# Decoder layer on one core: x squared by contiguous adds two groups later, FFN2's first gate/up group in row form

## Chip, cores and metric

One core of a Trainium2 chip. The metric is device time in microseconds of one execution, lower is better.

## What is computed

One decoder layer on x of 256 tokens by 1024 features, float32. Each sub-layer is wrapped in RMSNorms:

```python
x = x + 0.5 * rmsnorm(swiglu(rmsnorm(x, g1), w_gate, w_up, w_down), g2)      # FFN1, 2816 wide
x = x + rmsnorm(concat(attention(h), pooling(h)) @ w_out, g)                 # mixer
x = x + rmsnorm(cross_attention(h, rmsnorm(mem, gm)) @ wo, g)                # 4 heads
x = x + 0.5 * rmsnorm(swiglu(rmsnorm(x, g3), w_gate, w_up, w_down), g4)      # FFN2, 2816 wide
# swiglu: (silu(h @ w_gate) * (h @ w_up)) @ w_down
```

The root of the norm ahead of a product is one factor for each token. The kernel multiplies the unnormalised x (times the gain) and applies the root to the result, so a group of products can start before the root is known.

## The kernel before, in words

**Split weights.** Every weight and every x is split in a high half (rounded to fp32r) and a low half (the rest), and a product is three matmuls: hi by hi, lo by hi, hi by lo. Weights arrive in the order of use, in units of eight 128x128 tiles (512 KB), loaded by SP, mostly two to a transfer, into one of four `wraw` buffers (L66). `_make` (L70) casts a unit on ScalarE (`whi`, L76) and subtracts on VectorE (`wlo`, L77). `get` (L120) hands the next tiles to TensorE and, at the start of unit u, makes all units up to u + 4 (`LEAD`), or as many as `pace` says. There are six `whi` and six `wlo` buffers.

**Two forms of product.** In column form a weight tile is stationary and x (256 tokens, or 512 columns of hi and lo side by side) streams: `group` (L219) computes two gate and two up chunks (f = 0 and 1) in two PSUM banks, k by k, twelve matmuls of 256 columns for each of eight k; `gate_up` (L564) computes a later f, one unit for the gate and one for the up half, each eight pairs of 256 and 512 columns (L574, L575). In row form a 128x128 piece of x is stationary and 512 columns of weights stream: `row_product` (L293), three matmuls at L298 to L300.

**Order.** TensorE runs in program order everywhere. Between `seam(True)` and `seam(False)` (L795) all engines do; elsewhere a planner arranges the other engines.

**Opening.** `start` (L469) loads x and the first four units in parts and splits them (L108, L111, L181, L184). Then it squares x in place on ScalarE (L497, two halves) and reduces over the chunks on VectorE, reading with a stride (L498), and computes four small factors (L500). FFN1's `group` follows, then f = 2, 3, ... `x_sums` (L514) reduces over the partitions by four matmuls against a column of ones (eight TensorE instructions) after the gate of f = 2, and takes the root. `opened` (L604), after the gate of f = 3, spreads the root over the partitions (L286, two matmuls, four instructions) and finishes the f so far: root, silu, product, split into `h`. Down steps begin after f = 5. `mem_rows` (L526) is a load of SP's queue, issued after f = 4, into the buffer that held x.

**Seam ahead of FFN2.** The cross-attention's output product ends with three units (`row_end`, L368; `row_sums`, L313): tile t = 0 (128 tokens) of both 512-wide halves, then t = 1. Each half's result is squared and summed on ScalarE (L324) and scaled into `y` on VectorE (L327). `row_root` (L336) takes the root, `row_add` (L345) adds y to x (`xt`), `x_turn` (L349) transposes 128x128 pieces of `xt` on TensorE (L353), and `x_hi` (L374, ScalarE) and `x_lo` (L378, VectorE) split them. With no filler work (`fillers` empty, this seam only) the transposes of t = 0 stand after the products, `middle` and `ahead` do the first chunks, and `before(j)` puts the transposes of t = 1 and the other splits between the k of FFN2's first `group`. There `rows_square` (L507) sums x squared for the root, `x_root` (L356) follows at f = 3 and `opened` at f = 4. One `wlo` is made on GpSimd.

Of the kernel before, what the change touches and what calls it, by code (L numbers as in the profile page):

```python
# [47 lines left out]
class Weights:  # L48
# [33 lines left out]
    def open_in_parts(self, n_units, load, split):  # L82
# [54 lines left out]
def build(nc, io, tiles_only=False):  # L137
# [230 lines left out]
    def row_end(parts, ks, weights, factor, nxt, pre, fillers):  # L368
# [12 lines left out]
        def products():  # L381
            st["w"].pace = [(LEAD, None)] * (LATE - 1) + [(LEAD - 1, None)]
# [9 lines left out]
            box["sums"] = row_sums(parts, ks, ws, 1, factor, box["later"])  # L392
            x_turn(0, range(4), small)
            x_turn(0, range(4, 8), small)

        def middle():
            r = box["r"] = row_root(box["sums"])
            if not fillers:
                x_hi(0, 0)
                row_add(1, slice(0, P), r)  # L400
                x_hi(0, 1)
                return
            for c in range(ND):
                x_hi(0, c)
            for i in range(2):
                row_add(1, quarter(i), r)
            box["later"][0]()
            for i in range(2, 4):
                row_add(1, quarter(i), r)
            for c in range(4):  # L410
                x_lo(0, c)
# [13 lines left out]
        def ahead():  # L425
            r = box["r"]
            x_turn(1, (0,), accum)
            row_add(1, slice(P, S), r)
            x_lo(0, 0)
            x_turn(1, (1,), accum)  # L430
            x_hi(1, 0)
            x_hi(1, 1)
            row_add(1, quarter(1), r)
            x_lo(1, 0)
            x_lo(0, 1)
            x_lo(1, 1)
            box["later"][0]()

        def before(j):
            if fillers and j == 1:  # L440
                k_flush()
            if j == 0 and not fillers:
                st["w"].pace = [(2, "dve"), (2, "pool"), (2, "dve"), (3, "dve"), (3, None), (3, None)]
            if j % 2 == 1 and j < 7 and not fillers:
                c = j + 1
                x_turn(1, (c, c + 1), accum)
                for k in (c, c + 1):
                    x_hi(0, k)
                    x_hi(1, k)
                if c < 6:  # L450
                    row_add(1, quarter(c // 2 + 1), box["r"])
                for k in (c, c + 1):
                    x_lo(0, k)
                    x_lo(1, k)
            if j in (2, 4, 6, 7):
                rows_square(st["xt"], st["xsum"], {2: 0, 4: 1, 6: 2, 7: 3}[j])

# [5 lines left out]
        if not fillers:  # L463
            pr.add(ahead)
        return before
# [3 lines left out]
    def start():  # L469
# [43 lines left out]

    def x_sums():  # L514

        ps = small("sums")
        for t in range(2):
            for i in range(2):
                nc.tensor.matmul(ps[:, t:t + 1], st["xsq"][:, i, t * P:(t + 1) * P], st["one"],
                                 start=i == 0, stop=i == 1)  # L520
# [40 lines left out]
    def ffn(n, X, before, aside, last):  # L561
# [40 lines left out]
        first = 2 if n == 1 else 3  # L602

        def opened():  # L604
            x_spread()
            for f, t in enumerate(early):
                finish(f, t)
# [6 lines left out]
        group([wg, wu] * 2, X, [0, 0, P, P], early.extend, before=before, hi_first=n == 1)  # L614
        seam(False)
        for f in range(2, NF):
            gate, up = gate_up(f, early.append if f < first + 1 else lambda t, f=f: finish(f, t))
            pr.add(*gate)
            if f == first:
                side(x_sums if n == 1 else x_root)  # L620
            if f == first + 1:
                side(opened)
            pr.add(*up)
# [504 lines left out]
```

## Time and profile before

| | us |
|---|---|
| three runs | 577.92, 578.73, 578.73 |
| median | 578.73 |
| the profiled execution | 580.79 |
| its span | 578.6 |
| TensorE busy (matmuls) | 565.5 (98%) |
| VectorE busy | 411.2 (71%) |
| ScalarE busy | 341.6 (59%) |
| DMA engines, mean share | 53% |

The durations come from the profiled execution. A matmul's duration contains its passage through the array, so the distance between the starts of two matmuls, not the duration, is what one of them costs. Lines are those of the kernel before.

### The profile page before, as it was taken

The page shows a single profiled execution, that of the slowest core. Times are in us where ns is not written, and L with a number is a line of the kernel's source. Part 1 is how long each engine was busy: PE and PEld are TensorE (multiplying, and loading weights), DVE is VectorE, ACT ScalarE, POOL GpSimd, SP SyncE. Part 2 cuts the span into 40 slices and gives each one's busy share as a digit, 9 for nine tenths or more (in the row PEclk, how much of TensorE's full clock was granted, in tenths as well). Part 3 has the DMA queues.
Part 4 walks back from the last instruction along what each step waited for, and adds up shares of the span by engine and source line. Part 5 has one row for each costly group of instructions (what it writes and reads, how often), then busy time and mean ns, then how long its engine had stood idle before and what let it go on. Part 6 is the DMA issues. An engine that isn't in the chain of part 4 may idle for free.

```text
span 578.6 us, 8485 instructions
## 1 busy us (share of the span) xinstructions
PE 565.5 (98%) x3304; PEld 496.7 (86%) x3304; DVE 411.2 (71%) x662; ACT 341.6 (59%) x613; POOL 20.0 (3%) x37
## 2 busy tenths in 40 slices
PE   8799999999999999999999999999999999999995
PEld 8788888888888899988899988879888888888884
DVE  5898666787776678984568676467796766766654
ACT  6588575555555656775359456358674555555543
POOL 0000000000000000450000000001000000000001
PEclk9899999999999999999999999999999999999998
DMA  8885686645646068264256624426655555545202
GB/s 298 310 344 182 254 281 227 217 159 206 204 163 216 18 237 287 79 218 147 72 187 246 219 113 146 146 72 222 253 195 184 202 180 185 200 164 218 74 1 73
DMA packets 29400, 107.04 MB, mean 185 GB/s; under 512 B 2096, under 2 KB 3248, under 8 KB 28976
## 3 DMA queue, kind: packets, MB, share of 16 engines
q1 hardware_dynamic: 28928, 106.14, 52.3%
q8 instruction: 26, 0.43, 0.3%
q10 hardware_dynamic: 432, 0.35, 0.2%
q14 instruction: 14, 0.11, 0.0%
HBM read 105.44 MB, written 1.05 MB: 184 GB/s over the span
## 4 chain that ended last, share of the span: by engine, by line
PE 92%; DVE 3%; DMA 2%; ACT 1%; issue 1%; DVEq 0%; SPq 0%
PE acc L575 13%; PE sm L575 13%; PE acc L298 10%; PE acc L300 9%; PE acc L299 9%; PE acc L574 7%; PE sm L574 7%; PE acc L173 3%; PE acc L174 3%; PE acc L175 3%; PE acc L234 2%; PE acc L232 2%; PE acc L260 2%; PE acc L262 2%; PE acc L261 2%; PE acc L227 2%
## 5 line engine op out<-in xcount | busy, mean ns | idle before, releaser
L77 DVE TENSOR_TENSOR wlo<-wraw,whi 128x1024 fp32r<-128x1024 f32 x183 | 223.7, 1231 | 76.9 <-ACT whi L76 76.4
L76 ACT CAST whi<-wraw 128x1024 fp32r<-128x1024 f32 x184 | 192.5, 1053 | 51.1 <-PE acc L300 41.5
L575 PE MATMUL acc<-xs,whi 128*128 128x512 f32 x320 | 115.9, 401 | 0.0
L575 PE MATMUL sm<-xs,whi 128*128 128x512 f32 x320 | 114.5, 398 | 0.0
L574 PE MATMUL acc<-xs,wlo 128*128 128x256 f32 x320 | 90.4, 282 | 3.1 <-DVE wlo L77 3.1
L574 PE MATMUL sm<-xs,wlo 128*128 128x256 f32 x320 | 90.1, 282 | 0.0
L575 PEld LDWEIGHTS acc<-xs,whi 128*128 128x128 f32 x320 | 60.7, 190 | 14.6
L575 PEld LDWEIGHTS sm<-xs,whi 128*128 128x128 f32 x320 | 60.1, 188 | 14.9
L298 PE MATMUL acc<-whi,h 128*128 128x512 f32 x176 | 69.0, 392 | 0.0
L300 PE MATMUL acc<-whi,h 128*128 128x512 f32 x176 | 68.7, 390 | 0.0
L299 PE MATMUL acc<-wlo,h 128*128 128x512 f32 x176 | 68.5, 389 | 0.0
L574 PEld LDWEIGHTS acc<-xs,wlo 128*128 128x128 f32 x320 | 60.8, 190 | 4.5 <-DVE wlo L77 3.3
L574 PEld LDWEIGHTS sm<-xs,wlo 128*128 128x128 f32 x320 | 60.5, 189 | 0.0
L579 ACT COPY cmb<-acc 128x256 f32<-128x256 f32 x40 | 14.9, 373 | 53.6 <-PE acc L575 53.4
L173 PE MATMUL acc<-xs,wlo 128*128 128x256 f32 x160 | 46.1, 288 | 0.0
L174 PE MATMUL acc<-xs,whi 128*128 128x256 f32 x160 | 45.2, 283 | 0.0
L175 PE MATMUL acc<-xs,whi 128*128 128x256 f32 x160 | 45.2, 283 | 0.0
L579 ACT COPY cmb<-sm 128x256 f32<-128x256 f32 x40 | 14.8, 371 | 50.6 <-PE sm L575 50.6
L300 PEld LDWEIGHTS acc<-whi,h 128*128 128x128 f32 x176 | 33.0, 188 | 7.3
L299 PEld LDWEIGHTS acc<-wlo,h 128*128 128x128 f32 x176 | 33.1, 188 | 7.1
L298 PEld LDWEIGHTS acc<-whi,h 128*128 128x128 f32 x176 | 33.0, 188 | 5.6
L232 PE MATMUL acc<-xs,whi 128*128 128x256 f32 x128 | 32.4, 285 | 0.8 <-ACT whi L108 0.8
(179 smaller groups left out, 896.5 us busy)
## 6 DMA issues: line engine op xcount, KB each, us to landing
wraw<-w SPq DMA_DIRECT2D x91, 1024.0 KB, 4.8
post<-post SPq DMA_DIRECT2D x4, 512.0 KB, 5.2
wraw<-w SPq DMA_DIRECT2D x7, 256.0 KB, 5.8
wraw<-w SPq DMA_DIRECT2D x2, 512.0 KB, 7.2
y<-memt SPq DMA_DIRECT2D x1, 1024.0 KB, 9.9
y<-mem SPq DMA_DIRECT2D x1, 1024.0 KB, 6.9
xt<-xt SPq DMA_DIRECT2D x1, 1024.0 KB, 6.8
out_dram<-y SPq DMA_DIRECT2D x4, 128.0 KB, 1.9
```

The lines of the kernel that those rows point to most:

```text
L76: self.nc.scalar.copy(hi, raw)
L77: eng.tensor_tensor(lo, raw, hi.bitcast(F32), op=ALU.subtract)
L173: nc.tensor.matmul(o, lo, X[:, :S], start=first, stop=False, skip_group_check=True)
L174: nc.tensor.matmul(o, hi, X[:, :S], start=False, stop=False, skip_group_check=True)
L175: nc.tensor.matmul(o, hi, X[:, S:], start=False, stop=last, skip_group_check=True)
L232: nc.tensor.matmul(o[i], hi, st[X][:, k, :S], start=first and i % 2 == 0, stop=False, skip_group_check=True)
L298: nc.tensor.matmul(o, a, hi, start=first, stop=False, skip_group_check=True)
L299: nc.tensor.matmul(o, a, lo, start=False, stop=False, skip_group_check=True)
L300: nc.tensor.matmul(o, b, hi, start=False, stop=last, skip_group_check=True)
L574: nc.tensor.matmul(ps[:, S:], lo, x[:, :S], start=k == 0, stop=False, skip_group_check=True)
L575: nc.tensor.matmul(ps, hi, x, start=False, stop=k == ND - 1, skip_group_check=True)
L579: nc.scalar.copy(c, ps[:, S:])
```

## The change

1. `start` no longer squares x. `x_squares` does so after the gate of f = 2 of FFN1: the same two squares, then three contiguous adds that halve the chunks (8 to 4 to 2 to 1) in place. `x_sums` then needs half as many matmuls and moves behind the gate of f = 3, `opened` behind that of f = 4.
2. FFN2's first group becomes `row_group`: row form, first all k for t = 0, then all k for t = 1, into two PSUM banks that hold 128 tokens by gate and up of 256 features. Its four units are made ahead of the output products (`pace`), for which the `whi` and `wlo` pools get a seventh buffer; units behind it are made by `ahead` in its second half. The root of x is taken inside it (`late(2)`).
3. The eight transposes of t = 0 go between the last output products (`between`), those of t = 1 ahead of k = 6 of the first half and of the second half.
4. `row_h` applies root, silu and product in row form; `turn_h` turns the result back with four transposes after the gate of f = 5.
5. GpSimd no longer makes a unit.

The other two seams, which have fillers, keep their order. The diff, cut to its core:

```diff
+    def ahead(self, n):
+        while self.made <= min((self.pos - 1) // UNIT + n, self.n_units - 1):
+            self._make(self.made)
+            self.made += 1
...
-    def row_sums(parts, ks, ws, t, factor, later=None):
+    def row_sums(parts, ks, ws, t, factor, later=None, between={}):
...
                 row_product(parts(k), st["acc"], 0, False, j == len(ks) - 1, t, d, w)
+                if (i, j) in between:
+                    between[i, j]()
...
         def products():
-            st["w"].pace = [(LEAD, None)] * (LATE - 1) + [(LEAD - 1, None)]
+            st["w"].pace = [(LEAD, None)] * (LATE - 1) + [(LEAD - 1 if fillers else LEAD, None)]
...
-            box["sums"] = row_sums(parts, ks, ws, 1, factor, box["later"])
-            x_turn(0, range(4), small)
-            x_turn(0, range(4, 8), small)
+            between = {} if fillers else {(1, i): lambda i=i: turn_first(i) for i in range(2)}
+            box["sums"] = row_sums(parts, ks, ws, 1, factor, box["later"], between)
+            if fillers:
+                for i in range(2):
+                    x_turn(0, range(4 * i, 4 * i + 4), small)
+
+        def turn_first(i):
+            x_turn(0, range(4 * i, 4 * i + 4), small)
+            if i == 0:
+                for c in range(3):
+                    x_hi(0, c)
...
+            for c in range(4):
+                x_lo(0, c) if c < 3 else (x_hi(0, c), x_lo(0, c))
+            box["r"] = row_root(box["sums"])
...
+        def early(k):
+            r = box["r"]
+            if k == 0:
+                for c in range(4, ND):
+                    x_hi(0, c)
+                for i in range(2):
+                    row_add(1, quarter(i), r)
+                x_lo(0, 4)
+                box["later"][0]()
+                for c in range(5, ND):
+                    x_lo(0, c)
+                for i in range(2, 4):
+                    row_add(1, quarter(i), r)
+                for i in range(2):
+                    rows_square(st["xt"], st["xsum"], i)
+            if k == 6:
+                x_turn(1, range(4), small)
+                for c in range(4):
+                    x_hi(1, c)
+                for c in range(4):
+                    x_lo(1, c)
+
+        def late(k):
+            if k == 0:
+                x_turn(1, range(4, 8), small)
+                for c in range(4, 8):
+                    x_hi(1, c)
+                for c in range(4, 8):
+                    x_lo(1, c)
+                for i in range(2, 4):
+                    rows_square(st["xt"], st["xsum"], i)
+            if k == 2:
+                x_root()
+            if k in (1, 3, 5):
+                st["w"].ahead(k // 2 + 1)
...
-        st["xsq"] = tmp([P, 2, S], "q")
-        for i in range(2):
-            x = st["xf"][:, 4 * i:4 * i + 4, :]
-            nc.scalar.activation(x, x, AF.Square)
-            nc.vector.tensor_reduce(st["xsq"][:, i, :], x.rearrange("p c s -> p s c"), axis=AX.X, op=ALU.add)
...
+    def x_squares():
+        for i in range(2):
+            x = st["xf"][:, 4 * i:4 * i + 4, :]
+            nc.scalar.activation(x, x, AF.Square)
+        n = ND
+        while n > 1:
+            n //= 2
+            x = st["xf"][:, :n, :]
+            nc.vector.tensor_tensor(x, x, st["xf"][:, n:2 * n, :], op=ALU.add)
...
-            for i in range(2):
-                nc.tensor.matmul(ps[:, t:t + 1], st["xsq"][:, i, t * P:(t + 1) * P], st["one"],
-                                 start=i == 0, stop=i == 1)
+            nc.tensor.matmul(ps[:, t:t + 1], st["xf"][:, 0, t * P:(t + 1) * P], st["one"], start=True, stop=True)
...
-        first = 2 if n == 1 else 3
+        first = 3 if n == 1 else 2
...
+        def row_group(early, late):
+            def run():
+                st["w"].pace = [(3 - i, None) for i in range(4)]
+                ws = [st["w"].get(4) for _ in range(ND)]
+                ps = [accum() for _ in range(2)]
+                for t, ahead in enumerate((early, late)):
+                    for k, (hi, lo) in enumerate(ws):
+                        ahead(k)
+                        a = st[X][:, k, t * P:(t + 1) * P]
+                        b = st[X][:, k, S + t * P:S + (t + 1) * P]
+                        nc.tensor.matmul(ps[t], a, hi, start=k == 0, stop=False)
+                        nc.tensor.matmul(ps[t], a, lo, start=False, stop=False)
+                        nc.tensor.matmul(ps[t], b, hi, start=False, stop=k == ND - 1)
+                st["rows"] = ps
+                st["w"].pace = [(n, None) for n in (2, 2, 3, 3, 3)]
...
+        def row_h():
...
+                nc.scalar.activation(g, ps[:, :S], AF.Silu, scale=r)
+                nc.vector.scalar_tensor_tensor(g, ps[:, S:], r, g, op0=ALU.mult, op1=ALU.mult)
...
+        def turn_h():
...
+                    nc.tensor.transpose(ps[:, c * S + t * P:c * S + (t + 1) * P],
+                                        st["hrow"][t][:, c * P:(c + 1) * P], st["ident"])
...
+            if f == 2 and n == 1:
+                side(x_squares)
+            if f == first and n == 1:
+                side(x_sums)
             if f == first + 1:
                 side(opened)
+            if f == 5 and n == 2:
+                side(turn_h)
...
-              tc.tile_pool(name="hi", bufs=LEAD + 2) as hi,
-              tc.tile_pool(name="lo", bufs=LEAD + 2) as lo,
+              tc.tile_pool(name="hi", bufs=LEAD + 3) as hi,
+              tc.tile_pool(name="lo", bufs=LEAD + 3) as lo,
```

## Rows read from the trace of the kernel before

**Rows 1.** Waits of TensorE: line <- what ended the wait: us in total, times, longest

```profile
PE acc L574 <- DVE wlo L77: 3.1, 1, 3.1
PE acc L353 <- DVE xt L347: 0.9, 1, 0.9
```

**Rows 2.** Opening in order of time: start us, us, engine, line, operation [idle before <-releaser]

```profile
14.44 2.00 ACT L497 ACTIVATE y<-y 128x1024 f32<-128x1024 f32 x2
15.53 3.95 DVE L498 TENSOR_REDUCE q<-y 128x256 f32<-128x1024 f32 x2
...
17.20 0.64 PE L227 MATMUL acc<-xs,wlo 128*128 128x256 f32 x4
...
19.46 2.00 ACT L76 CAST whi<-wraw 128x1024 fp32r<-128x1024 f32 x2 [1.14 <-DMA wraw<-w]
19.63 4.62 DVE L77 TENSOR_TENSOR wlo<-wraw,whi 128x1024 fp32r<-128x1024 f32 x4
20.91 0.39 PE L574 MATMUL acc<-xs,wlo 128*128 128x256 f32 x1 [3.06 <-DVE wlo L77]
...
24.70 0.56 SPq L503 DMA_DIRECT2D y<-memt  x1
24.95 1.38 PE L519 MATMUL sums<-one,q 128*128 128x1 f32 x8
...
29.09 0.28 PE L574 MATMUL acc<-xs,wlo 128*128 128x256 f32 x1
...
30.05 9.09 SPq L66 DMA_DIRECT2D wraw<-w  x3
...
31.92 0.61 PE L286 MATMUL pb<-const,rcx 128*128 128x128 f32 x4
...
32.28 0.36 PE L574 MATMUL sm<-xs,wlo 128*128 128x256 f32 x1
```

**Rows 3.** Stretches of the opening: busy us by engine, granted clock, DMA share, GB/s

```profile
17.80:20.90 3.10, 0.04 (x1) 0.00 (x0) 3.10 (x7) 1.96 (x3) 0.00 (x0) 1.00 0.69 279
...
22.40:24.90 2.50, 2.50 (x9) 2.15 (x8) 1.86 (x2) 0.00 (x0) 0.00 (x0) 0.51 0.92 372
```

**Rows 4.** SP's issues of unit 4, and of units 8 and 9, in order of time

```profile
7.51 0.43 SPq L66 DMA_DIRECT2D wraw<-w  x1
...
15.52 0.38 SPq L66 DMA_DIRECT2D wraw<-w  x1
```

**Rows 5.** Those two issues in the DMA view: KB each, us to landing

```profile
wraw<-w SPq DMA_DIRECT2D x1, 512.0 KB, 6.8
...
wraw<-w SPq DMA_DIRECT2D x1, 1024.0 KB, 6.4
```

**Rows 6.** Seam ahead of FFN2 in order of time, TensorE

```profile
371.70 0.39 PE L300 MATMUL acc<-whi,xs 128*128 128x512 f32 x1
...
383.26 0.39 PE L300 MATMUL acc<-whi,xs 128*128 128x512 f32 x1
383.49 1.04 PE L353 MATMUL sm<-const,xt 128*128 128x128 f32 x8
...
398.44 0.28 PE L574 MATMUL acc<-xs,wlo 128*128 128x256 f32 x1
```

**Rows 7.** Stretch after the output products, columns as in rows 3

```profile
383.49:385.40 1.91, 1.03 (x9) 0.80 (x7) 0.63 (x3) 1.50 (x5) 0.00 (x0) 1.00 0.00 0
```

**Rows 8.** Groups from 383.4 to 400 by shape: count | busy us, mean ns | idle before

```profile
L374 ACT ACTIVATE xs<-sm,gain 128x128 fp32r<-128x128 f32 x8 | 2.8, 365 | 0.4 <-DVE xs L378 0.4
L378 DVE SCALAR_TENSOR_TENSOR xs<-sm,gain,xs 128x128 fp32r<-128x128 f32 x8 | 2.8, 345 | 2.3 <-ACT xs L374 2.2
L511 ACT ACTIVATE q<-xt 128x512 f32<-128x512 f32 x4 | 2.6, 640 | 0.0
L347 DVE SCALAR_TENSOR_TENSOR xt<-y,fs,xt 128x256 f32<-128x256 f32 x3 | 1.4, 479 | 0.0
L327 DVE SCALAR_TENSOR_TENSOR y<-acc,post 128x512 f32<-128x512 f32 x1 | 0.7, 682 | 0.0
```

More of the change, by code (lines that the diff above doesn't have):

```diff
@@ L391, in products @@
             box["later"] = []
-            box["sums"] = row_sums(parts, ks, ws, 1, factor, box["later"])
-            x_turn(0, range(4), small)
-            x_turn(0, range(4, 8), small)
-        def middle():
[L397 to L401, printed above, removed]
-                return
-            for c in range(ND):
-                x_hi(0, c)
-            for i in range(2):
[L406 to L409, printed above, removed]
+            between = {} if fillers else {(1, i): lambda i=i: turn_first(i) for i in range(2)}
[8 more added lines that the diff above has]
+                    x_hi(0, c)
+        def middle():
+            if fillers:
+                r = row_root(box["sums"])
+                for c in range(ND):
+                    x_hi(0, c)
[6 more added lines that the diff above has]
+                    x_lo(0, c)
+                return
             for c in range(4):
-                x_lo(0, c)
+                x_lo(0, c) if c < 3 else (x_hi(0, c), x_lo(0, c))
+            box["r"] = row_root(box["sums"])
         def turned(i):
@@ L423, in turned @@
             return run
[L425 to L437, printed above, removed]
         def before(j):
-            if fillers and j == 1:
+            if j == 1:
                 k_flush()
[L442 to L454, printed above, removed]
@@ L455, in before @@
             if j in (2, 4, 6, 7):
                 rows_square(st["xt"], st["xsum"], {2: 0, 4: 1, 6: 2, 7: 3}[j])
+        def early(k):
+            r = box["r"]
+            if k == 0:
+                for c in range(4, ND):
+                    x_hi(0, c)
+                for i in range(2):
+                    row_add(1, quarter(i), r)
+                x_lo(0, 4)
+                box["later"][0]()
+                for c in range(5, ND):
+                    x_lo(0, c)
+                for i in range(2, 4):
+                    row_add(1, quarter(i), r)
+                for i in range(2):
[6 more added lines that the diff above has]
+                    x_lo(1, c)
@@ L458, in row_end @@
+        def late(k):
[5 more added lines that the diff above has]
+                    x_lo(1, c)
+                for i in range(2, 4):
+                    rows_square(st["xt"], st["xsum"], i)
[3 more added lines that the diff above has]
+                st["w"].ahead(k // 2 + 1)
         pr.add(products, weights)
@@ L462, in row_end @@
             pr.add(turned(i))
-        if not fillers:
-            pr.add(ahead)
-        return before
+        return before if fillers else (early, late)
     def start():
@@ L512, in rows_square @@
                              accum_out=sums[:, t, half:half + 1])
+    def x_squares():
+        for i in range(2):
+            x = st["xf"][:, 4 * i:4 * i + 4, :]
[5 more added lines that the diff above has]
+            nc.vector.tensor_tensor(x, x, st["xf"][:, n:2 * n, :], op=ALU.add)
     def x_sums():
@@ L606, in opened @@
             for f, t in enumerate(early):
-                finish(f, t)
+                finish(f + (2 if n == 2 else 0), t)
+        def row_group(early, late):
[13 more added lines that the diff above has]
+                st["w"].pace = [(n, None) for n in (2, 2, 3, 3, 3)]
+            pr.add(run, [(n, k * P, c * P) for k in range(ND) for n in (wg, wu) for c in range(2)])
+        def row_h():
+            st["hrow"] = []
+            for t, ps in enumerate(st["rows"]):
+                r = st["rx"][:, t:t + 1]
+                g = st["ffn"].tile([P, S], F32, name="hrow", bufs=2)
+                nc.scalar.activation(g, ps[:, :S], AF.Silu, scale=r)
+                nc.vector.scalar_tensor_tensor(g, ps[:, S:], r, g, op0=ALU.mult, op1=ALU.mult)
+                st["hrow"].append(g)
+        def turn_h():
+            ps = small("ht")
+            for c in range(2):
+                for t in range(2):
+                    nc.tensor.transpose(ps[:, c * S + t * P:c * S + (t + 1) * P],
+                                        st["hrow"][t][:, c * P:(c + 1) * P], st["ident"])
+            for c in range(2):
+                h = st["h", c] = st["ffn"].tile([P, 1, 2 * S], F32R, name="h", bufs=LAG + 4)
+                split_plain(h, 0, ps[:, c * S:(c + 1) * S])
         def down(k):
@@ L612, in down @@
             pr.add(lambda: row_step(st["h", k], 0, k == 0), [(wd, k * P, c * P) for c in range(ND)])
-        group([wg, wu] * 2, X, [0, 0, P, P], early.extend, before=before, hi_first=n == 1)
+        if n == 1:
+            group([wg, wu] * 2, X, [0, 0, P, P], early.extend, before=before, hi_first=True)
+        else:
+            row_group(*before)
         seam(False)
+        if n == 2:
+            side(row_h)
         for f in range(2, NF):
```

3 lines of the change are left out of this document (removed).

## The prediction

> **What bounds the kernel now.** I read the list of waits first: it names what TensorE stood still for. It is short. One wait of 3.1 us for VectorE's `wlo` (L77) at L574 is by far the longest; the next that the change touches is 0.9 us at the transposes of L353 [rows 1]. Everywhere else TensorE is fed, so an edit to another engine is worth nothing unless it reaches one of these places, and what TensorE itself executes counts in full. Then I read both places in the order of time.
>
> In the opening, FFN1's first group ends with four L227 matmuls that start at 17.20; their x4 lasts 0.64 us, one lasts 0.28, so a 256-column matmul starts every 0.12 us and the next line is due at 17.20 + 4 x 0.12 = 17.68. It starts at 20.91 [rows 2]. What VectorE does in that time stands just above: the two tensor_reduce of x squared hold it from 15.53 to 19.48, and only at 19.63 does it begin the low halves of the weights [rows 2]. ScalarE's two squares begin at 14.44 and take 2.00 us, ahead of the casts. The second cost is behind the stall: the granted clock is 1.00 to 22.4 and then 0.51 until 24.9 [rows 3], that is the 1.2 GHz level and not 2.4 GHz, after an engine that had worked 0.04 us in 3.1.
>
> At the seam in front of FFN2 the last output product starts at 383.26, eight transposes follow at 383.49, and the next gate/up pair (f = 2) starts at 398.44 [rows 6]. The first group, 16 transposes and the wait for the normalised x lie in those 14.95 us. TensorE is busy 1.03 of the first 1.91 us, and the clock stays 1.00 [rows 7].
>
> **Part 1, the squares.** Removed from the opening: two squares on ScalarE (2.00 us) and two reduces on VectorE (3.95 us). What is late next? Unit 4 is the first that f = 2 needs. Its load is issued at 7.51 and lands 6.8 us later, at 14.3 [rows 4, 5]. Its cast can begin when ScalarE is through with the opening, about 14.5 (where the squares began), and takes half of the 2.00 us that two take: 15.5. VectorE is free at 15.53, does the four tiny operations on `half` (some 0.3 us, they stood behind the reduces), then one of its four low halves, 4.62 / 4 = 1.16 us: 17.0 [rows 2]. That is 0.7 us ahead of 17.68, so the wait goes entirely. Unit 6 is the one that waits for its data at 19.46 now [rows 2]; cast and low half end by 21.7, and it is needed at 17.68 + two units. A unit of f = 2 and later is eight pairs from 29.09 to 31.92, 2.83 us [rows 2], so at 23.3: no new wait.
>
> The sum: (a) 20.91 - 17.68 = 3.23 us. (b) From 20.91 to 29.09 TensorE now takes 8.18 us for two units and the eight L519 matmuls of `x_sums`. At the clock of the stretch behind, the units take 5.66. `x_sums` is halved to four: the nearest row is the four L286 matmuls of the spread, 31.92 to 32.28, 0.36 us; bounds are 0.2 and, half of what lies there now, 0.69. So 8.18 - 5.66 - 0.36 = 2.16 us. Together 5.39. I count on the clock staying at 1.00, because the gap that came before the fall is gone.
>
> Added, two units later: the same squares (2.00) and three adds of 1024, 512 and 256 elements. By a 1024-wide VectorE row, 1.16 us, in proportion and with some start cost, 1.2 + 0.7 + 0.4 = 2.3 us. `x_sums` needs them when f = 3's gate ends, 17.68 + 3 x 2.83 = 26.2. ScalarE has cast units 6 and 7 at 21.46, and the copy of f = 2's gate (0.4) may come before the squares: 23.9. The adds, with another VectorE step between them, end at 26.2 to 26.6. TensorE runs in order, so any lateness counts: I take 0.2, bounds 0 and 2.1 (rival A). **Opening: 5.2 us gained, bounds 3.1 and 5.6.**
>
> The queue: `mem_rows` writes the buffer in which x was squared and must now wait for `x_sums`. It was issued at 24.70, and SP's next weight load went out at 30.05 [rows 2]; the new earliest time, about 26.5, is still ahead of that, so nothing behind it in SP's order is late. Cost 0; if the cover were gone, a load lands 6 to 7 us after issue [rows 5] against a lead of four units, 11 us. `opened` of FFN1 goes one f later, 31.9, and h of unit 0 is needed at the first down step, after f = 5, three units on: 8.5 us for four finishes. FFN2 does exactly this now, and the list of waits has none there. Cost 0, bound 0.5.
>
> **Part 2, the seam.** TensorE's work after the last product now: 16 transposes and 48 matmuls of 512 columns in place of 96 of 256. The same form, 512 columns of weights over a 128 x 128 piece of x, starts at 371.70 and, 51 starts later, at 383.26: 0.2267 us each [rows 6]. So 48 x 0.2267 = 10.88, against 96 x 0.12 = 11.52 now: 0.64 gained by the form. Eight transposes take 1.04 us with a last one of 0.27, so 0.11 each [rows 6]; 16 are 1.76. The work is 12.64 us where 14.95 pass now. Eight of the transposes move into the products; they cost the same there, but no longer need cover, since `row_add` of tile 0 is done before they are reached (the wait that is left in the chain is for tile 1).
>
> The Trainium skill prices the form otherwise: TensorE: Matmul & The Clock Gate, section Back-to-back issue gap, gives N/2.4 + 2.5 ns as the isolated gap. By it 96 x 109.2 and 48 x 215.8 ns are 10.48 and 10.36 us, so the row form would gain 0.12, and the sum below would be 5.9. The rows differ on both forms (120 and 227 ns), so I go by them.
>
> What could still hold TensorE there, counted from the last product, E: its square ends at E + 0.9, then x_hi of chunk 3, the root (0.3), x_hi 4 to 7 at 0.37, x_lo at 0.345, four row_add at 0.48, the deferred `y` at 0.68 [rows 8]. VectorE's line is x_lo 3 (to 1.75), reciprocal (1.9), two row_add (2.9), x_lo 4 (3.2), y (3.9), x_lo 5 (4.25). TensorE wants x_lo 4 at 4 x 0.68 + 0.45 = 3.17 and x_lo 5 at 3.85: 0.4 us late in all, the `y` in between being the cause. Chunks 6 and 7 and the second tile come in time, since TensorE has eight transposes to do (row_add ends at 5.9, TensorE asks at 6.3).
>
> Then the weights. All four units of the group are made before the products; that puts one cast earlier into a place where ScalarE now waits for a buffer, so it costs nothing, and the seventh buffer is what allows it. The price is paid behind: units 4 to 6 are made inside the second half of the group, after x_hi and four squares (0.64 and a 0.2 read each). By full durations the first cast ends at E + 11.1 and its low half at 12.4, and TensorE asks at 12.64 + 0.4 = 13.0. The next cast stands behind the root's reduce on VectorE and ends at 14.0, its low half at 15.2; asked for at 15.9. It fits with 0.6 us to spare, so I take 0.15 for hand-overs.
>
> Added: `turn_h`, four transposes at 0.11 = 0.44 on TensorE (bounds 0.4, and 1.1 by the pace of single ones, 0.27). `row_h` runs beside f = 2 on the other engines and removes two 128 x 512 multiplies from VectorE. **Seam: 14.95 - 12.64 - 0.4 - 0.15 - 0.44 = 1.3 us gained, bounds -0.5 and 1.9.** The negative end is one row_add and one cast more on the path than counted.
>
> **Sum.** 5.2 + 1.3 = 6.5 us. The profiled execution took 580.79 us with a span of 578.6; the median of the runs is 578.73, 2.06 below. The terms are differences within the span, so I take them off the median: **572.2 us**.
>
> **Rivals.** A, *`x_sums` waits for the squares.* If the casts of units 8 and 9 go ahead of the squares on ScalarE: that load is issued at 15.52 and lands 6.4 later at 21.9 [rows 4, 5]; with one cast in front the adds end at 27.3, with two at 28.3, so TensorE stands 1.1 to 2.1 us at 26.2. Time 573.3 to 574.3. For it: the cast's instruction is written first. Against: now those two casts run after the root that follows `x_sums`. Chance 0.17.
>
> B, *a new wait at the end of the row group.* Three makes in 5 us behind eight x_hi and two squares; if a cast slips by 2 us the seam gains nothing: 573.5. For it: 0.6 us of slack only. Chance 0.13; A and B together, 575.2, 0.03.
>
> D, *the row form runs at the pace of the gate/up pairs.* There 768 columns take 0.354 us, so 512 take 0.236 and the form gains 0.19: 572.7. Against: 52 starts of the very form [rows 6]. Chance 0.05. The formula of the Trainium skill (TensorE: Matmul & The Clock Gate, Back-to-back issue gap) points the same way, with 0.12.
>
> E, *the opening waits for data anyway.* Were unit 4 there only at 16.35, one unit later than by its landing, 0.9 us of the wait stays: 573.1. Against: its landing at 14.3. Chance 0.03.
>
> C, *slower.* In the opening a stop of 3.1 us was followed by a clock of 0.51 [rows 3]. The new group hands x over chunk by chunk in its first 5 us; if TensorE's pauses there come to such a stop, the 10.88 us of the group could run at half clock and cost up to 10.9 more: 583. It decides against the change where more than 6.5 us of work run at that level. Against: the seam now has a 0.9 us wait and a clock of 1.00 [rows 1, 7], and the pauses that I count are 0.4. Chance 0.05, of which 0.02 ends near no change.
>
> **How the numbers follow.** The forecast with its small terms (571.3 to 573.0) has 0.54. The low end: no lateness in either place and the cheap ends of `x_sums` and `turn_h`, 0.2 + 0.55 + 0.2 below, and 0.5 for the seventh buffer elsewhere: 570.7. The high end takes in A, B and their sum: 575.3. About 0.12 lies outside. A measurement of this kernel tells 0.2%, 1.2 us, from no change: faster 0.95, same 0.02, slower 0.03.
>
> **What would show it.** Right: no L574 wait near 18 us, a granted clock of 1.00 from 5 us on, f = 2 of FFN1 near 17.7; between the last product and f = 2 of FFN2 about 13.2 us less the eight transposes that now lie ahead (12.3); four transposes at f = 5. Wrong: a wait at `x_sums` (A), at the first L574 of FFN2 (B), a spacing of 0.236 in the group (D), a clock of 0.5 behind the seam (C).

## The result and the profile after

| | before | after |
|---|---|---|
| median of six runs on the same chip, us | 579.55 (577.92 to 581.13) | 575.74 (574.22 to 576.18) |
| ratio, 95% interval | | 0.9921 (0.9901 to 0.9940) |
| profiled execution, us | 580.79 | 575.60 |
| its span, us | 578.6 | 573.8 |
| TensorE busy, us | 565.5 | 564.7 |

Faster by 4.6 us by the ratio (3.5 to 5.7), 3.8 by the medians. Forecast were 6.5. On the median that the prediction started from, 578.73, the ratio gives 574.2: inside the range, 2 us above the point. Before's median is higher here than the 578.73 known ahead because the three runs that joined took 580.4 to 581.1 us. The median after by itself, 575.74, lies 0.4 above the range's end of 575.3.

TensorE's waits in the profile after, the whole list. Both waits of [rows 1] are gone:

```profile
PE warm L507 <- DVE cmb L504: 1.2, 1, 1.2
PE acc L238 <- ACT whi L108: 0.7, 1, 0.7
PE acc L240 <- DVE xs L386: 0.5, 2, 0.3
```

The opening after, in order of time (start us, us, engine, line). L233 is L227 of before, L603 L574, L549 L519, L538 and L543 are the squares and the adds:

```profile
7.55 1.05 PE L233 MATMUL acc<-xs,wlo 128*128 128x256 f32 x4
...
13.02 0.64 PE L233 MATMUL acc<-xs,wlo 128*128 128x256 f32 x4
...
15.31 1.06 ACT L538 ACTIVATE y<-y 128x1024 f32<-128x1024 f32 x1 [0.38 <-DVE xs L190]
...
16.41 1.22 DVE L543 TENSOR_TENSOR y<-y 128x1024 f32<-128x1024 f32 x1 [0.28 <-ACT y L538]
...
17.55 2.35 DVE L77 TENSOR_TENSOR wlo<-wraw,whi 128x1024 fp32r<-128x1024 f32 x2
...
19.26 0.28 PE L603 MATMUL acc<-xs,wlo 128*128 128x256 f32 x1
...
27.75 0.50 PE L549 MATMUL sums<-one,y 128*128 128x1 f32 x4
```

Two things differ from what I had worked out. The four L233 at 7.55 take 1.05 us; four of the same matmuls in the trace of before take 0.64. Two starts from that trace's slow stretch stand behind them:

```profile
7.10 0.64 PE L227 MATMUL acc<-xs,wlo 128*128 128x256 f32 x4
...
23.03 0.41 PE L574 MATMUL acc<-xs,wlo 128*128 128x256 f32 x1
23.24 0.63 PE L575 MATMUL acc<-xs,whi 128*128 128x512 f32 x1
```

Up to about 10.2 us the 256-column matmuls of the changed kernel start every 0.213 us; in before they start every 0.12 from 5.5 us on. In the stretch of [rows 3] with a granted clock of 0.51 the 256-column matmul at 23.03 takes as long, 0.21 us to the next start, so 0.213 is the 1.2 GHz level. The first group ends at 19.26 and not at 17.68. And the squares (the first at 9.78) and the first add, "two groups later" in the code, run *ahead* of unit 4's cast and low half: the planner drew them into the opening. The clock behind it stays up, as forecast (compare the second row of [rows 3]):

```profile
22.40:24.90 2.50, 2.50 (x15) 2.14 (x14) 2.42 (x4) 2.16 (x3) 0.00 (x0) 1.00 0.99 383
```

The seam after, TensorE in order of time. L304 is the first product, L650 the row group, L671 `turn_h`:

```profile
372.02 0.39 PE L304 MATMUL acc<-whi,xs 128*128 128x512 f32 x1
...
378.82 0.60 PE L361 MATMUL sm<-const,xt 128*128 128x128 f32 x4
...
381.10 0.39 PE L650 MATMUL acc<-whi,xs 128*128 128x512 f32 x1
...
382.25 0.39 PE L652 MATMUL acc<-whi,xs 128*128 128x512 f32 x1
...
384.98 0.40 PE L652 MATMUL acc<-whi,xs 128*128 128x512 f32 x1
...
392.96 0.28 PE L603 MATMUL acc<-xs,wlo 128*128 128x256 f32 x1
...
412.99 0.60 PE L671 MATMUL ht<-const,hrow 128*128 128x128 f32 x4
413.35 0.36 PE L603 MATMUL sm<-xs,wlo 128*128 128x256 f32 x1
```

From the first output product to f = 2 it is 20.94 us; before it was 23.12 (that product started at 375.32, f = 2 in [rows 6]). The row group runs without a pause: twelve starts from 382.25 to 384.98, 0.228 us each.

### The profile page after: what moved, and what is told of

Its sections match the earlier page's. It is cut to its first block, busy times and chain, and to the rows that moved or that the text cites. A ratio compares the mean times of both kernels' runs of the same rounds, so it can differ in the third digit from the quotient of the medians.

```text
span 573.8 us, 8367 instructions
## 1 busy us (share of the span) xinstructions
PE 564.7 (98%) x3256; PEld 494.2 (86%) x3256; DVE 408.8 (71%) x661; ACT 343.2 (60%) x615; POOL 17.3 (3%) x36
## 3 DMA queue, kind: packets, MB, share of 16 engines
HBM read 105.44 MB, written 1.05 MB: 186 GB/s over the span
## 4 chain that ended last, share of the span: by engine, by line
PE 86%; DVE 9%; ACT 3%; issue 1%; DMA 1%; DVEq 0%; SPq 0%; ACTq 0%
PE acc L604 13%; PE sm L604 12%; PE acc L306 10%; PE acc L304 10%; PE acc L305 9%; PE acc L603 6%; PE sm L603 6%; DVE wlo L77 3%; PE acc L266 2%; PE acc L268 2%; PE acc L267 2%; PE acc L240 2%; PE acc L238 2%; PE acc L180 1%; PE acc L179 1%; PE acc L181 1%
## 5 line engine op out<-in xcount | busy, mean ns | idle before, releaser
L603 PE MATMUL sm<-xs,wlo 128*128 128x256 f32 x320 | 90.2, 282 | 0.0
L603 PE MATMUL acc<-xs,wlo 128*128 128x256 f32 x320 | 89.8, 281 | 0.0
L304 PE MATMUL acc<-whi,h 128*128 128x512 f32 x176 | 69.0, 392 | 0.0
L603 PEld LDWEIGHTS acc<-xs,wlo 128*128 128x128 f32 x320 | 60.4, 189 | 1.3
L603 PEld LDWEIGHTS sm<-xs,wlo 128*128 128x128 f32 x320 | 60.5, 189 | 0.0
L180 PE MATMUL acc<-xs,whi 128*128 128x256 f32 x160 | 45.2, 283 | 0.0
L181 PE MATMUL acc<-xs,whi 128*128 128x256 f32 x160 | 45.2, 283 | 0.0
L304 PEld LDWEIGHTS acc<-whi,h 128*128 128x128 f32 x176 | 33.0, 188 | 5.6
L609 DVE TENSOR_TENSOR gu<-acc,cmb 128x256 f32<-128x256 f32 x40 | 16.9, 423 | 21.0 <-ACT cmb L608 21.0
```

The costliest lines, as they stand in the source:

```text
L180: nc.tensor.matmul(o, hi, X[:, :S], start=False, stop=False, skip_group_check=True)
L181: nc.tensor.matmul(o, hi, X[:, S:], start=False, stop=last, skip_group_check=True)
L304: nc.tensor.matmul(o, a, hi, start=first, stop=False, skip_group_check=True)
L603: nc.tensor.matmul(ps[:, S:], lo, x[:, :S], start=k == 0, stop=False, skip_group_check=True)
L609: nc.vector.tensor_tensor(box[0][:, s, :], ps[:, :S], c, op=ALU.add)
```

## The experiments

Every kernel's trace was cut at the same starts of TensorE matmuls. The first output product is the first of the 36 matmuls that end the cross-attention's output product; the last column ends where the first matmul of FFN2's last product starts. This table carries most of what follows (us):

| kernel | f = 2 of FFN1 | its wait there | first output product | that to FFN2's f = 2 | FFN2's f = 2 to its last product |
|---|---|---|---|---|---|
| before, first trace | 20.91 | 3.1 | 375.32 | 23.12 | 172.89 |
| before, second trace | 20.55 | 1.0 | 373.25 | 23.13 | 172.89 |
| seven buffers | 20.32 | 2.7 | 373.41 | 23.11 | 172.89 |
| opening alone | 18.59 | 0.3 | 370.89 | 23.12 | 172.89 |
| seam alone | 20.15 | 0.7 | 373.28 | 20.92 | 173.54 |
| changed, first trace | 19.26 | 0 | 372.02 | 20.94 | 173.54 |
| changed, second trace | 18.23 | 0.4 | 370.86 | 20.94 | 173.55 |
| written order | 19.32 | 0 | 375.72 | 20.94 | 173.55 |
| squares in the middle | 17.68 | 0 | 370.47 | 20.91 | 173.52 |
| transposes behind | 18.75 | 0.3 | 371.41 | 21.78 | 173.54 |
| reduces | 19.19 | 0 | 372.31 | 20.92 | 173.52 |
| changed, ten warm-up matmuls | 18.22 | 0.3 | 370.89 | 20.92 | 173.53 |
| written order, ten | 17.99 | 0 | 374.38 | 20.92 | 173.56 |
| squares in the middle, ten | 17.75 | 0 | 370.56 | 20.92 | 173.52 |

From FFN2's f = 2 on, kernels with the same seam agree within 0.04 us; what differs from one trace of a kernel to the next lies in the opening (before's two traces are 2.00 us apart at 34 us and 2.07 at the first output product).

### Both kernels once more

No edit.

> The kernel before, unchanged, looked at once more. Question: in the first trace of the changed kernel the first 33 matmuls of FFN1's group (5.7 to 10.1 us) start every 0.21 us and only then every 0.12; in the trace of before they run at 0.12 from 5.5 us on. Theory A: where TensorE's clock rises in the opening differs from one execution to the next, whatever the kernel; then this look may as well show the rise near 10 us, and its span lies 1.5 us or more above the first look's if so. Theory B: the change causes it (squares among the opening's casts); then this look shows the rise near 5.3 us again. Both expect the 3.1 us wait at L574 and the fall of the clock behind it.

Measured: 578.74 us, span 576.6. The 256-column matmuls start every 0.213 us up to about 9.5 us:

```profile
8.30 1.05 PE L227 MATMUL acc<-xs,wlo 128*128 128x256 f32 x4
```

TensorE's wait, VectorE's reduces and low halves, `x_sums`, and two stretches (columns as in rows 3) of that execution:

```profile
PE acc L574 <- DVE wlo L77: 1.0, 1, 1.0
...
15.07 4.05 DVE L498 TENSOR_REDUCE q<-y 128x256 f32<-128x1024 f32 x2
...
19.25 4.65 DVE L77 TENSOR_TENSOR wlo<-wraw,whi 128x1024 fp32r<-128x1024 f32 x4
...
23.48 0.95 PE L519 MATMUL sums<-one,q 128*128 128x1 f32 x8
...
20.50:22.40 1.90, 1.85 (x10) 1.64 (x11) 1.90 (x2) 0.00 (x0) 0.00 (x0) 1.00 0.49 47
22.40:25.00 2.60, 2.60 (x19) 2.39 (x18) 2.09 (x4) 0.85 (x3) 0.00 (x0) 1.00 0.98 399
```

So the kernel before has the slow first matmuls too: theory A. (The changed kernel's first trace has some 20 of them, not the 33 of the expectation.) But what both theories expected behind them is not there: the wait is 1.0 us instead of 3.1, no fall of the clock follows, and the span is 2.1 us shorter, not longer. Yet f = 2 starts at nearly the same time, 20.55 against 20.91. VectorE's low half sets that start (19.25 plus one of four, 1.16, and the hand-over), not TensorE; when TensorE comes later, it waits less. Of the 2.07 us that the first trace is longer, 0.35 lie at f = 2 and 1.6 in the two units behind it, where it has the fall of the clock [rows 3].

> The changed kernel, unchanged, looked at once more and timed. Theory A expects a late rise of the clock in some executions only; where it rises near 5.3 us the first group ends near 17.7 to 18.0, and then the low half of unit 4, which ended at 18.7 in the first trace, makes TensorE wait 0.7 to 1.1 us at f = 2. Theory B expects the slow first matmuls again, and the first group's end near 19.3. Time: 4 to 5 us below before by the first set of runs.

Measured: 574.87 us, ratio 0.9927 (0.9910 to 0.9944), span 572.6. Here the clock rose near 6.5 us. The first group ended in time, and unit 4's low half was late, by 0.4 us where 0.7 to 1.1 was expected:

```profile
7.08 0.64 PE L233 MATMUL acc<-xs,wlo 128*128 128x256 f32 x4
...
PE acc L603 <- DVE wlo L77: 0.4, 1, 0.4
...
16.96 2.35 DVE L77 TENSOR_TENSOR wlo<-wraw,whi 128x1024 fp32r<-128x1024 f32 x2
```

Second trace against second trace the change gains 2.32 us up to f = 2, next to nothing from there to the seam (352.70 against 352.63 us, in which `x_sums` is 0.45 shorter), and 1.53 from the first output product on: 3.9 in all, the size of the ratio.

### Each part alone, and the seventh buffer

*Opening alone*: the kernel before with part 1. *Seam alone*: the changed kernel with

```diff
+        st["xsq"] = tmp([P, 2, S], "q")
+        for i in range(2):
...
-    def x_squares():
...
-        first = 3 if n == 1 else 2
+        first = 2
...
-            if f == 2 and n == 1:
-                side(x_squares)
```

(cut; squares, reduces and four matmuls in `x_sums` as before.)

*Seven buffers*: before with `bufs=LEAD + 3` for `whi` and `wlo`.

> Part 1 alone on the kernel before: squares by adds behind f = 2, half the matmuls of x_sums, roots one f later; the seam ahead of FFN2 as before. By my prediction's terms 5.2 us below before. By the first trace of the changed kernel 3.7 us were gained by 34 us, of which 1.6 were lost to the late rise of the clock; so 3.5 to 5.2. If the loss between 34 and 372 us (0.4 us in that trace) came from the seventh buffer, it is absent here.

> Part 2 alone: the changed kernel with the squares and reduces put back into the opening and x_sums after f = 2's gate. My prediction: 1.3 us below before. By the first trace of the changed kernel the seam from the first output product to f = 2 took 20.94 us against 23.11, 2.17 gained, less 0.4 for the transposes of f = 5: 1.75. If the seventh buffer costs something elsewhere: 1.3.

> The kernel before with seven instead of six weight buffers and nothing else. In the traces of both kernels with the seam's change 0.2 to 0.4 us are lost between 190 and 250 us against the kernels with six, part of it regained by 380. If the buffer does that, this kernel is 0 to 0.3 us above before; if the seam's gain comes from the buffer (casts earlier), it is 1 us or more below.

Measured: opening alone 577.06 us, 0.9959 (0.9946 to 0.9972), 2.4 us; seam alone 576.88, 0.9968 (0.9955 to 0.9982), 1.9 us; seven buffers 579.20, 1.0008 (0.9995 to 1.0020). The two parts add up to the whole (0.9927). The opening's 2.4 us (1.6 to 3.1) lie below the 3.5 to 5.2 expected. By its trace the seam gains 23.13 - 20.92 = 2.2 us, less 0.65 in FFN2 behind it: 1.55, inside the interval of the 1.9 (1.0 to 2.6). The seventh buffer gains nothing: by the ratio that kernel is 0.5 us above before (-0.3 to 1.2). From f = 2 to the first output product it takes 353.09 us against 352.70. The other traces without a fall of the clock make the same two groups once the shorter `x_sums` (0.45) is added back, 352.75 with six buffers and 353.1 to 353.25 with seven, so part 2 pays about 0.4 us for it in the middle of the kernel. 0.2 to 0.3 of it are lost near 248 us, at self-attention's transposes (L689); what they wait for there was not followed up. The trace with seven buffers shows one thing more: TensorE waits 2.7 us at f = 2, and the clock does not fall behind it:

```profile
PE acc L574 <- DVE wlo L77: 2.7, 1, 2.7
...
22.40:25.00 2.60, 2.60 (x20) 2.39 (x19) 1.86 (x4) 1.12 (x3) 0.00 (x0) 1.00 0.95 384
```

### The squares where the code writes them

```diff
-            nc.scalar.activation(x, x, AF.Square)
+            st["tc"].keep_in_program_order(nc.scalar.activation(x, x, AF.Square))
...
-            nc.vector.tensor_tensor(x, x, st["xf"][:, n:2 * n, :], op=ALU.add)
+            st["tc"].keep_in_program_order(nc.vector.tensor_tensor(x, x, st["xf"][:, n:2 * n, :], op=ALU.add))
```

> The changed kernel with its two squares and three adds kept in the written order, so that the engines do them behind f = 2's gate as the change describes. In the changed kernel the planner had drawn them into the opening: the second square and the 1024-wide add run ahead of unit 4's cast and low half. Theory A2 (the two engines' order in the opening sets f = 2's start where the clock rises early): unit 4's low half ends about 17.1 instead of 18.2, no wait of TensorE there where the first group ends at 17.8, so 0.4 us less in such an execution and nothing where the clock rises late: 0 to 0.4 us below the changed kernel. Rival A of my prediction: TensorE waits at x_sums, up to 1.1 us, which makes it slower by up to 1 us.

Measured: 579.38 us, ratio 0.9991 (0.9977 to 1.0006): the whole gain of the change is gone, where 0.4 us less to 1 us more than the changed kernel was expected. TensorE's waits, the chain that made them, and the stretch behind:

```profile
PE sums L549 <- DVE y L543: 1.3, 1, 1.3
...
PE sm L603 <- ACT rt L284: 0.4, 1, 0.4
...
22.62 2.01 ACT L538 ACTIVATE y<-y 128x1024 f32<-128x1024 f32 x2
24.53 1.99 ACT L76 CAST whi<-wraw 128x1024 fp32r<-128x1024 f32 x2
...
24.66 1.22 DVE L543 TENSOR_TENSOR y<-y 128x1024 f32<-128x1024 f32 x1 [1.48 <-ACT y L538]
25.80 1.22 DVE L77 TENSOR_TENSOR wlo<-wraw,whi 128x1024 fp32r<-128x1024 f32 x1
26.94 0.68 DVE L543 TENSOR_TENSOR y<-y 128x512 f32<-128x512 f32 x1
27.54 1.22 DVE L77 TENSOR_TENSOR wlo<-wraw,whi 128x1024 fp32r<-128x1024 f32 x1
28.67 0.42 DVE L543 TENSOR_TENSOR y<-y 128x256 f32<-128x256 f32 x1
...
29.24 0.58 PE L549 MATMUL sums<-one,y 128*128 128x1 f32 x4 [1.28 <-DVE y L543]
...
30.20:33.50 3.30, 3.27 (x10) 2.89 (x11) 3.02 (x5) 1.85 (x2) 0.00 (x0) 0.50 0.69 241
```

The squares begin behind f = 2's gate. VectorE does a weight's low half of 1.22 us after the first add and another after the second, so the last add ends at 29.1, and TensorE, due at `x_sums` 1.3 us earlier, stands. It stands 0.4 us more behind `x_sums`, and then the granted clock is 0.50 for 3.3 us: the next unit takes 4.41 us (30.23 to 34.64), against 2.90 in the changed kernel's first trace. So the wait of the prediction's rival A is real and of the size that was worked out, but it comes another way: A had the casts of units 8 and 9 ahead of the squares on ScalarE, and here they come behind (24.53); it is two low halves between the adds on VectorE that make it. That the changed kernel is free of it is the planner's doing.

### More warm-up

```diff
-        for _ in range(8):
+        for _ in range(10):
             nc.tensor.matmul(ps[:, :P], warm[:, :P], warm[:, :P], start=True, stop=True)
```

> The changed kernel with ten instead of eight warm-up matmuls ahead of the first group, so that TensorE has no gap between them (end at 4.97 now) and its first product (5.1 to 6.5). If that gap is what leaves the clock at the lower level until 9.5 to 10.3 us in some executions, the rise comes near 5 to 7 us in all, the first group ends by 18 us, and the median falls by up to 1 us, with a smaller spread. If the rise depends on the time of the start alone, it stays at 9.5 or 10 in some and nothing changes; the two matmuls may then push the first products back by up to 0.8 us, which the wait for unit 4 hides in part.

> Both: written order of the squares and ten warm-up matmuls. If both theories hold, f = 2 starts near 17.8 in every execution, against 18.2 to 19.3 for the changed kernel: 0.4 to 1.5 us less, median about 1 us below the changed kernel. If neither, no change.

Measured: with the changed kernel 574.80, 0.9922 (0.9906 to 0.9939); with the written order 577.77, 0.9962 (0.9949 to 0.9975). In the first the clock rose near 4.8 us, but f = 2 started at 18.22, as in the second trace of the changed kernel: the low half is what it waits for, so an earlier clock buys nothing there. The second has f = 2 at 17.99 and the same 1.3 us wait at `x_sums` with the same fall of the clock. Whether the two matmuls move the rise was not settled: with ten it came at 4.8, 6.4 and 5.4 us (the third kernel follows below), with eight between 4.9 and 10.3 over eleven traces, by 6.5 us in six of them.

### The squares where ScalarE is idle

```diff
-            group([wg, wu] * 2, X, [0, 0, P, P], early.extend, before=before, hi_first=True)
+            group([wg, wu] * 2, X, [0, 0, P, P], early.extend, before=lambda k: x_squares() if k == 4 else None,
+                  hi_first=True)
...
-            if f == 2 and n == 1:
-                side(x_squares)
```

> The changed kernel with the squares and adds written behind unit 5's cast inside FFN1's first group, where ScalarE waits for unit 6's data anyway. If the gain of the opening is decided by what stands ahead of unit 4's low half: that ends near 17.2 instead of 18.2, TensorE does not wait at f = 2 (0.3 to 0.4 us in the changed kernel where the clock rises early), x_sums waits for nothing, as the adds end by 21.5: 0 to 0.4 us below the changed kernel. If moving the squares at all brings TensorE to x_sums too early, as in the kernel with the written order: a wait there and 1 to 4 us more.

> The same with ten warm-up matmuls. With nothing late on VectorE, f = 2 starts when the first group ends, so now an early rise of the clock in every execution should count: f = 2 at 17.8 to 18.0 in all, 0.3 to 0.5 us below the kernel with the squares in the middle where that one's clock rises late in some. If the rise is not moved by the two matmuls: the same time.

Measured: 573.97 us, 0.9918 (0.9900 to 0.9936), and with ten warm-up matmuls 574.26, 0.9920 (0.9902 to 0.9937). Three rows of the first one:

```profile
15.13 2.36 DVE L77 TENSOR_TENSOR wlo<-wraw,whi 128x1024 fp32r<-128x1024 f32 x2
...
16.07 2.00 ACT L538 ACTIVATE y<-y 128x1024 f32<-128x1024 f32 x2
...
17.68 0.28 PE L603 MATMUL acc<-xs,wlo 128*128 128x256 f32 x1
```

Unit 4's low half comes first, the squares fill the time in which ScalarE waits for unit 6's data, and f = 2 starts at 17.68, what the prediction had worked out from [rows 2] (that it is so to the digit is chance: 17.75 with ten warm-up matmuls). It is 0.55 us earlier there than the second trace of the changed kernel, and 0.4 at the seam. The ratio can't tell that from the changed kernel's 0.9927; by these traces it is the better version. Ten warm-up matmuls add nothing to it.

### Reduces in the new place

```diff
+        st["xsq"] = tmp([P, 2, S], "q")
...
-        n = ND
-        while n > 1:
-            n //= 2
-            x = st["xf"][:, :n, :]
-            nc.vector.tensor_tensor(x, x, st["xf"][:, n:2 * n, :], op=ALU.add)
+            nc.vector.tensor_reduce(st["xsq"][:, i, :], x.rearrange("p c s -> p s c"), axis=AX.X, op=ALU.add)
```

(with the former four matmuls in `x_sums`.)

> The changed kernel with the two strided reduces in place of the three adds (and four instead of two matmuls in x_sums), the planner free as in the change. It tells the form of the sum from its place: VectorE does 3.95 us of reduces instead of 2.3 us of adds. If the contiguous form decides, unit 4's or unit 5's low half comes late again by 1 us or more and the time is 1 to 2 us above the changed kernel. If the place decides (no reduce ahead of unit 4's low half), f = 2 starts as early as in the changed kernel and only x_sums is longer, 0.4 us: within 0.6 us.

Measured: 575.76 us, 0.9943 (0.9923 to 0.9962). By the ratios that is 0.9 us above the changed kernel, between the 0.6 that was the bound if the place decides and the 1 to 2 if the form does. By the trace, f = 2 starts at 19.19 without a wait, like the first trace of the changed kernel (its clock rose near 10.0 too), and `x_sums` takes 0.81 us instead of 0.36. The planner puts one reduce in a gap and the other behind unit 4's low half, which ends at 18.0, ahead of the first group's end in this trace:

```profile
16.76 1.22 DVE L77 TENSOR_TENSOR wlo<-wraw,whi 128x1024 fp32r<-128x1024 f32 x1
17.89 2.06 DVE L540 TENSOR_REDUCE q<-y 128x256 f32<-128x1024 f32 x1
```

So the place gives the start of f = 2; the form gives the 0.45 us of `x_sums`. Where the other half of the 0.9 lies, this trace does not tell.

### Tile 0's transposes behind the products

```diff
-            between = {} if fillers else {(1, i): lambda i=i: turn_first(i) for i in range(2)}
+            between = {}
...
-            if fillers:
-                for i in range(2):
-                    x_turn(0, range(4 * i, 4 * i + 4), small)
+            for i in range(2):
+                x_turn(0, range(4 * i, 4 * i + 4), small)
+            if not fillers:
+                for c in range(3):
+                    x_hi(0, c)
```

> The changed kernel with tile 0's eight transposes put back behind the last output product instead of between the last ones; all else as changed. My prediction's reading: TensorE executes the same work, but the first split of x then ends later by 0.17 + 0.37 + 0.35 us and more, behind the last square on ScalarE: three x_hi and x_lo come after it, so the row group's first matmul waits about 1.0 us and its third product of each chunk follows VectorE's 0.27 to 0.35 us pace with a second stop: 1.0 to 1.8 us above the changed kernel. If the place of the transposes doesn't matter (the row form and the splits ahead do it all): within 0.3 us.

Measured: 576.02 us, 0.9944 (0.9927 to 0.9960). The seam takes 21.78 us instead of 20.93, and the pauses stand where expected, at the first product and at the first that needs a low half:

```profile
380.78 0.50 PE L652 MATMUL acc<-whi,xs 128*128 128x512 f32 x1 [0.16 <-ACT xs L382]
381.11 0.40 PE L653 MATMUL acc<-wlo,xs 128*128 128x512 f32 x1
381.68 0.50 PE L654 MATMUL acc<-whi,xs 128*128 128x512 f32 x1 [0.17 <-DVE xs L386]
```

0.85 us, somewhat under the 1.0 to 1.8 expected; the first pause is some 0.3 us and not 1.0. The place of the transposes is worth that much of the seam's 2.2. That the rest is the row form and the work ready ahead of it is argued; neither was run alone.

## Why the prediction was right or wrong

**The sign held, the way in the opening did not.** Both waits that were to go are gone, the two parts add, and no rival happened in the changed kernel. But its squares did not run two units later. The planner left them in the opening, and the gain came because VectorE had one add of 1.22 us ahead of unit 4's low half in place of 3.95 us of reduces. In the order that the prediction describes the gain is gone (0.9991), so that the sign came out is in part luck. The size was off, mostly by one step.

**The step that failed: "The terms are differences within the span, so I take them off the median."** They were differences to an execution that holds a cost which others of this kernel don't. I had noted that it lies 2.06 us above the median, and went on. The second trace shows what those 2 us are. In the first the clock rises early, the first group ends early, TensorE waits 3.1 instead of 1.0 us, and the clock falls to 0.51 behind that. In the second trace f = 2 starts 0.35 us earlier all the same. An early rise alone does not bring the fall: with seven buffers the clock rose at 5.1 us, the wait was 2.7 and the clock stayed up. Terms (a) and (b), 5.39 us, hold against the first trace only where the changed kernel's clock rises early as well and unit 4's low half is in time. In its own first trace the clock rose near 10.2 us (the sign "a granted clock of 1.00 from 5 us on" fails by the spacing) and 1.6 us of (a) went there; in the second trace, against before's second, (a) is 2.32 and (b) 0.57 (from `x_sums` 0.81 to 0.36, and the hand-over): 2.9 together.

**The second step: "Added, two units later: the same squares".** The forecast had unit 4's low half end at 17.0. The planner put a square and an add ahead of it, so it ended at 18.1 in the second trace, and f = 2 came with it. With the squares written into ScalarE's gap it came in time and f = 2 started at 17.68. Of the 2.3 us by which the opening's 2.9 falls short of the forecast 5.2 this is 0.55; the baseline is 1.94 (0.35 at f = 2, 1.59 in (b)), and the 0.2 taken for lateness at `x_sums` did not come. I had read from the order of before that the planner puts off a cast that waits for data, but not drawn the conclusion that it brings forward what waits for nothing.

**Rival A** I gave 0.17 at 1.1 to 2.1 us. In the changed kernel x_sums waits for nothing; where the order is kept it waits 1.3, inside what was worked out but by VectorE's low halves and not by ScalarE's casts, and the second pause and the fall of the clock behind it, not in that rival, bring the price to 3.7 (f = 2 to the first output product 356.41 us against 352.76).

**The seam** was sized at 1.3 and measured 1.5 from the first output product to the last product (196.02 against 194.49 us, second traces), 1.9 (1.0 to 2.6) as a part alone. Its terms err in both directions. From the last product's end to f = 2 it is 11.86 us (381.10 to 392.96) against 12.3: waits of 0.4 and 0.15 were forecast and none is there, because I summed whole durations where the split instructions follow each other closer (four `x_hi` take 1.14 us in the trace after, not 4 x 0.37). The form's 0.2267 us measured 0.228, so rival D with its 0.236 is out. By the formula of the Trainium skill for an isolated matmul (TensorE: Matmul & The Clock Gate, Back-to-back issue gap) the estimate is 0.216, which this trace does not agree with. (With the 0.12 that the prediction worked out from it, its sum would be 6.0 and not 5.9.) Eight transposes between products cost 0.92 (381.10 - 372.02, less 36 x 0.2267) against 0.88. `turn_h` took 0.36 against 0.44. Not seen was what follows it: the first down step needs the low half of `h` of unit 0, which VectorE now makes late, behind a weight's low half and another `h`. The third matmul of that step starts 0.53 us after the second in the second trace, not 0.23:

```profile
415.30 0.40 PE L305 MATMUL acc<-wlo,h 128*128 128x512 f32 x1
...
415.36 0.41 DVE L195 TENSOR_TENSOR h<-ht,h 128x256 fp32r<-128x256 f32 x1
...
415.83 0.50 PE L306 MATMUL acc<-whi,h 128*128 128x512 f32 x1
```

The twelve matmuls of that step take 3.19 us instead of 2.72 in before's second trace. These 0.47 us and `turn_h`, less some 0.2 that FFN2 gains ahead of them, are the 0.66 by which the last stretch of the table is longer. I had asked what waits for `turn_h`'s inputs and not who waits for its output.

**Covered at nothing.** `mem_rows` on SP and `opened` one f later: no wait of TensorE appears for either. The seventh buffer, for which the range allowed a gain of 0.5, costs about 0.4 between f = 2 and the first output product.

## What to carry to other kernels

Where the profiled execution lies above the median of the runs, find what it holds that the others don't before taking terms from it. Where another engine sets a start, the length of the wait says only how early TensorE came: count from what that engine sets. Read in the planned order where a moved instruction really lands: code that says "two groups later" ran ahead, and the written place costs the whole gain. Of a result that is moved or turned, ask who waits for the output and what stands in front on the engine that finishes it.

## What the runs showed of the hardware that was not expected

- The clock's rise in the opening differs between executions of the same kernel: near 5.4 and 9.5 us for before, 10.2 and 6.5 for the changed one, by the spacing of 0.213 and 0.12 us. The granted clock column reads 1.00 there throughout (also from 5 to 10 us in the changed kernel's first trace, at a spacing of 0.213), so in the first microseconds the spacing is the better witness.
- The fall of the clock does not follow from the length of a pause alone: after 3.1 us it fell (before, first trace), after 2.7 us it did not (seven buffers), after 1.3 us, the four one-column matmuls of `x_sums` and 0.4 us it fell (written order). What decides was not settled.
- The strided reduce of 1024 elements takes 2.0 us, 4.05 for two, and the contiguous add 1.22. The Trainium skill (VectorE: DVE Perf Modes, The perf-mode tier table) has both at the same rate in fp32, which these rows do not show. Its formula for the add, (N + 151)/0.96 ns (same page, The TRN2 errata), gives an estimate of 1.22, which agrees with the trace.
